# Probabilities times V as one FP32 matmul, new arena sizes, and grouped-query projections evacuated by ScalarE, in a two-layer hybrid encoder

## Chip, cores and metric

One core of one Trainium2 chip runs the whole program. The metric is device microseconds per execution. The kernel before takes 2137.96 us, the median of three runs (2136.34 to 2138.89).

## What is computed

Two groups of tokens (256 of a prompt and 512 of a sample, 768 columns in all) go through two layers with the same weights. Everything is FP32 at the interface. Cut to what matters here:

```python
for l in range(DEPTH):                       # DEPTH = 2, D_MODEL = 1024
    x = x + parallel_mixers(rmsnorm(x, norm_mix_g[l]), w_in[l], ...)    # 16 heads of 64
    x = x + memory_cross_attention(rmsnorm(x, norm_x_g[l]), mem, ...)   # 4 heads, 256 memory tokens
    x = x + conv_ffn(rmsnorm(x, norm_ffn_g[l]), ...)                    # gated MLP, width 2752

# parallel_mixers: 4 heads of dilated attention (A), 4 of mLSTM (B), 8 of grouped-query attention (C)
qc = axial_rope(rmsnorm(heads(c_q, C_HEADS), qk_g[0]), rope_row, rope_col)
kc = axial_rope(rmsnorm(heads(c_k, C_KV_HEADS), qk_g[1]), rope_row, rope_col)
s = einsum('bqkgd,bskd->bkgqs', q, k);  p = softmax(s);  o = einsum('bkgqs,bskd->bqkgd', p, v)
```

## The kernel before

Activations lie with channels on the partitions and the 768 tokens on the free axis. `STREAMS` is the order in which the two groups are worked on: `(256, 512)` first, then `(0, 256)` (first column, count). Almost all matmuls run in the type fp32r with both operands split into a high part (a rounding copy, usually by ScalarE, `hi_op`) and a low part (a DVE subtraction). A projection `proj` (`mm_chunks`, L213 to L215) makes three matmuls for each of 8 weight chunks: high by high, high by low, low by high. Its weights arrive by DMA in `wr` and are split into `wh` (ScalarE) and `wl` (DVE).

A layer is four stages in the program: the mixers, the output projection and cross attention, and the FFN (`up`, `down`; L1105 to L1107 and L1148 to L1150). In the mixers `ahead(first, second)` puts the projections of the next head group beside the attention of the present one; a scheduler that works on priorities and planned durations then sets the order of the instructions on every engine. Each engine takes its own list strictly in that order.

`attend` (L367 to L406) is one head of one group of tokens. Scores go to PSUM bank `s` (L378, L379; two banks), `soft` turns them to probabilities in a 512-column tile of `arena_f`, and PE transposes these 128 by 128 into bank `t` (L392; two banks). Then, for each `t` of 512 columns:

- ScalarE copies `t` to `ph` in fp32r (through L183), and DVE writes `pl` as `t` minus `ph` (through L158). Both lie in a small arena `asm` of 4 x 512 columns.
- PE multiplies by the tokens of V, whose tile holds for each head a [high, low] pair of 64 columns each (the second head of a pair has them the other way round): L400 with `ph`, L401 with `pl`, both into bank `yps`, of which there is one (tag `Y`). So 64 partitions of `yps` collect the high part of V and the other 64 the low part.
- At a head's end ScalarE copies one half of `yps` to the result row block and DVE adds the other half (`xall<-yps` and, in cross attention, `arena_f<-yps`).

There are 184 such `t` in the program. The V tiles come from `v_tokens` (L340 to L353): a transpose into `vps`, then for each of two heads a ScalarE copy (L350) and a DVE subtraction.

Of the grouped-query heads, `c_kv` (L582) and `c_q` (L627) project k and q. DVE evacuates PSUM with one operation (`ev_k`, `ev_q`): times the head's gain, times the row `rbc` of the layer norm (1/rms of each token, spread over the partitions). ScalarE squares the same PSUM for the per-head norm (L635 and L193); `head_rs` makes the reciprocal roots. `ones` and indicator columns multiply FP32 sums of squares on PE in `col_sums` (L268), one matmul for each 128 tokens: `col_sums` on 512 tokens issues four.

Two arenas in SBUF hand out tiles by hand: `arena_r` (fp32r; 18 x 768 columns and the 4 x 512 of `asm`) and `arena_f` (FP32; 18 x 768). A tile that was freed can be taken again, and the new writer waits for the old readers.

Of the kernel before, what the change touches and what calls it, by code (L numbers as in the profile page):

```python
# [44 lines left out]
R_COLS = 18 * 768  # L45
S_COLS = 4 * 512
PREP = 7 * 512
F_COLS = 18 * 768
# [60 lines left out]
def trunk_kernel(ctx, tc, xT, memT, w_in, w_out, w_xq, w_xkv, w_xo, w_up, w_dn, w_dnt, par, fin_g, cst, fmk, tabs,  # L109
# [18 lines left out]
    r_all = ap.tile([128, R_COLS + S_COLS], F32R, name="arena_r")  # L128
    ar = Arena(r_all, R_COLS, T)
    asm = Arena(r_all[:, R_COLS:], S_COLS)  # L130
# [23 lines left out]
    scr_v = nc.dram_tensor("scr_v", (DEPTH, 2, 128, 4 * 2 * 128), F32, kind="Internal").ap()  # L154
# [64 lines left out]
    C_G, A_G, SITE = [0], [0], [""]  # L219
# [147 lines left out]
    def attend(qs, q0, nq, KH, KL, k0, nk, vv, vt0, e, y, y0, soft, settle_p=None):  # L367
# [20 lines left out]
        for kb in range(0, nkt, nb):  # L388
# [17 lines left out]
        tt(yo, yps[64 * e:64 * e + 64, :n], yo, ALU.add)  # L406
# [59 lines left out]
    def kv_proj(l, mh, ml, arena, ftile, first, each=None):  # L466
        for j in range(4):
# [6 lines left out]
            hl = arena.tile(1024)  # L474
# [5 lines left out]
            else:  # L480
                vv = hl.rearrange("p (a b c) -> p a b c", a=2, c=128)
                v_tokens(z, 4, [vv[:, 0], vv[:, 1]], "kv%d" % l)
                SY.dma_start(out=scr_v[l, j - 2], in_=hl.bitcast(F32))
            arena.free(hl)
# [33 lines left out]
    def mixers(l, xt, x_dram, stats):  # L518
# [63 lines left out]
        def c_kv():  # L582
# [4 lines left out]
            def ev_k(ps, c0, n):  # L587
                stt(zk[:, c0:c0 + n], ps, pr[:, l, C_KG:C_KG + 1], rbc[:, c0:c0 + n], ALU.mult, ALU.mult)
# [30 lines left out]
        def v_proj(t):  # L619
            zv = ft()  # L620
            proj(w_in[l, t], xh, xl, ev_to(zv, "v%d" % t), sub="w_v%d" % t)
            vv = [rtl(), rtl()]
            v_tokens(zv, 6, [tok(v) for v in vv], "v%d" % t)
            af.free(zv)
            return vv

        def c_q(g):  # L627
            cosc, sinc = C["cos"], C["sin"]
            zs, sqs = [], []
            for a in range(2):  # L630
                z, sq = ft(), ft()

                def ev_q(ps, c0, n, z=z, sq=sq, a=a):
                    stt(z[:, c0:c0 + n], ps, pr[:, l, C_QG + a:C_QG + a + 1], rbc[:, c0:c0 + n], ALU.mult, ALU.mult)
# [10 lines left out]
            V.tensor_scalar(rq8, rq, 0.125, None, op0=ALU.mult)  # L645
# [23 lines left out]
        def c_attn(g, qr):  # L669
            C_G[0], SITE[0] = g, "c%d" % g  # L670
            qs, rq8 = qr
            K = C["k"][g]
            vv = C["v"][g]
# [6 lines left out]
            ar.free(K, vv)  # L680
# [53 lines left out]
        def b_attn(pb, sv):  # L734
            SITE[0] = "b%d" % pb
            sts, vv, rows = sv
            for e in range(2):
                qs, K = sts[e]
                hd = 2 * pb + e
                for c0, n in STREAMS:  # L740
                    gb = rows[e][:, 2 * c0:2 * c0 + 2 * n].rearrange("p (d k) -> p d k", d=2)
                    attend(qs, c0, n // 128, K[:, :T], K[:, T:], c0, n, tok(vv[e]), c0 // 128, e, yt[5 + pb], c0,
                           *b_soft(gb, c0, n, hd))
                af.free(rows[e])
                ar.free(qs, K, vv[e])
# [77 lines left out]
        def a_attn(pg, sv, order, last=True):  # L823
            A_G[0], SITE[0] = pg, "a%d" % pg
            sts, vv = sv
            for e, (c0, n) in order:
                qs, K = sts[e]
                attend(qs, c0, n // 128, K[:, :T], K[:, T:], c0, n, tok(vv[e]), c0 // 128, e, yt[4 + 3 * pg], c0,
                       mask_soft(C["fm"], den[:, 4 + pg, c0 // 128:(c0 + n) // 128, e]))
            if last:  # L830
                for e in range(2):
                    ar.free(*sts[e], vv[e])
# [611 lines left out]
```

## Time and profile before

| | |
|---|---|
| median of three runs | 2137.96 us |
| the profiled execution | 2145.01 us, of which the span of the trace is 2143.2 us |
| PE busy | 2003.8 us, 93% |
| PE weight loads busy | 1782.8 us, 83% |
| DVE busy | 1841.7 us, 86% |
| ScalarE (ACT) busy | 1061.7 us, 50% |
| granted PE clock, mean | 0.963 |
| chain that ended last | PE 74%, DVE 16%, ACT 4%, DMA 3%, issue 2% |

The profile puts each instruction on its engine's line with a start and a duration. Matmuls are pipelined: a record goes on after the next matmul has begun, so the distance of starts tells what a matmul costs PE, and the duration doesn't. PEclk is the share of the full TensorE clock that was granted. The first layer's mixers and cross attention lie between about 75 and 600 us, its FFN from there to 1085, the second layer's mixers and cross attention from 1085 to 1660, its FFN from 1660 to 2120.

### The profile page before, as it was taken

Reading aid. Unit: us, or ns where it says so; the run is one execution under the profiler, and the core shown is the slowest. Engines: PE = TensorE matmul, PEld = TensorE weight load, DVE = VectorE, ACT = ScalarE, POOL = GpSimd, SP = SyncE. Lnnn points to the kernel's source line nnn. Section 1 sums busy time; section 2 is a strip of 40 time slices with the busy share of each in tenths; the row PEclk is TensorE's granted clock in tenths of the full one; section 3 lists DMA queues with packets and bytes.
Section 4 is the critical chain, followed back from the end, with each engine's and each line's share of the span. In section 5 each row is a group of like instructions: output and inputs, shape, how many; then the busy total and the mean of one; then the engine's idle time right before and its main releaser. Section 6 shows DMA issues by size and latency. Waiting matters only on the chain.

```text
span 2143.2 us, 31059 instructions
## 1 busy us (share of the span) xinstructions
PE 2003.8 (93%) x11280; PEld 1782.8 (83%) x11280; DVE 1841.7 (86%) x3822; ACT 1061.7 (50%) x2119; POOL 7.8 (0%) x32
## 2 busy tenths in 40 slices
PE   7989989998899999999999897999988999999997
PEld 5878768787789999999888775777877999999995
DVE  8787887867999999999977868778779999999998
ACT  4257767547533333333534667565665333333342
POOL 0000000000000000000000000000000000000000
PEclk8989989999999999999999998999999999999998
DMA  5433335342132212212254314343421222222202
GB/s 179 138 82 101 96 89 124 110 132 80 50 90 79 67 62 72 74 63 88 65 179 117 92 44 107 99 111 123 124 64 56 83 70 69 70 69 70 69 30 79
DMA packets 62953, 190.94 MB, mean 89 GB/s; under 512 B 8072, under 2 KB 11400, under 8 KB 62032
## 3 DMA queue, kind: packets, MB, share of 16 engines
q1 hardware_dynamic: 62800, 188.96, 30.1%
q8 instruction: 89, 1.46, 0.3%
q14 instruction: 64, 0.52, 0.1%
HBM read 145.97 MB, written 10.71 MB: 73 GB/s over the span
## 4 chain that ended last, share of the span: by engine, by line
PE 74%; DVE 16%; ACT 4%; DMA 3%; issue 2%; SPq 1%; POOL 0%; DVEq 0%; ACTq 0%
PE rps L1105 8%; PE rps L1107 8%; PE rps L1106 8%; PE rps L1148 5%; PE rps L1149 5%; PE rps L1150 5%; PE prS L213 4%; PE prS L214 4%; PE prS L215 4%; DVE arena_f L158 4%; PE t L392 3%; PE prP L213 2%; PE prP L214 2%; PE prP L215 2%; DVE arena_r L158 2%
## 5 line engine op out<-in xcount | busy, mean ns | idle before, releaser
L158 DVE TENSOR_TENSOR arena_f<-arena_f 128x512 f32<-128x512 f32 (+2 forms) x373 | 265.6, 728 | 27.7 <-DMA arena_f<-arena_f 15.2
L183 ACT CAST wh<-arena_f 128x512 fp32r<-128x512 f32 x266 | 162.2, 621 | 253.0 <-PE rps L1106 212.8
L183 ACT CAST wh<-wr 128x512 fp32r<-128x512 f32 x260 | 159.4, 620 | 236.3 <-PE rps L1106 98.9
L158 DVE TENSOR_TENSOR xall<-rps,xall 128x512 f32<-128x512 f32 (+1 forms) x384 | 197.9, 549 | 14.1 <-PE rps L1150 6.9
L1148 PE MATMUL rps<-arena_r,wh 128*128 128x512 f32 (+1 forms) x608 | 202.6, 339 | 3.4 <-DVE xall L158 3.2
L158 DVE TENSOR_TENSOR wl<-wr,wh 128x512 fp32r<-128x512 f32 x264 | 179.5, 683 | 29.5 <-ACT wh L183 27.9
L1105 PE MATMUL rps<-xha,wh 128*128 128x384 f32 x608 | 203.9, 335 | 0.5 <-ACT wh L183 0.4
L1106 PE MATMUL rps<-xla,wh 128*128 128x384 f32 x608 | 203.4, 335 | 0.0
L1149 PE MATMUL rps<-arena_r,wh 128*128 128x512 f32 (+1 forms) x608 | 201.2, 338 | 0.0
L1107 PE MATMUL rps<-xha,wl 128*128 128x384 f32 x608 | 199.2, 334 | 0.0
L213 PE MATMUL prS<-xha,wh 128*128 128x512 f32 x480 | 188.8, 397 | 3.1 <-DVE arena_f L158 1.0
L215 PE MATMUL prS<-xha,wl 128*128 128x512 f32 x480 | 189.1, 396 | 1.5 <-DVE wl L158 1.5
L214 PE MATMUL prS<-xla,wh 128*128 128x512 f32 x480 | 189.9, 396 | 0.0
L158 DVE TENSOR_TENSOR wl<-arena_f,wh 128x512 fp32r<-128x512 f32 x266 | 179.2, 684 | 1.5 <-ACT wh L183 1.3
L1150 PE MATMUL rps<-arena_r,wl 128*128 128x512 f32 (+1 forms) x608 | 178.3, 339 | 0.0
L158 DVE TENSOR_TENSOR arena_f<-rps,arena_f 128x384 f32<-128x384 f32 x266 | 143.6, 552 | 28.2 <-PE rps L1107 26.0
L1105 PE MATMUL rps<-arena_r,wh 128*128 128x384 f32 x456 | 152.8, 335 | 0.0
L1106 PE MATMUL rps<-arena_r,wh 128*128 128x384 f32 x456 | 152.3, 334 | 0.0
L158 DVE TENSOR_TENSOR arena_r<-t,arena_r 128x512 fp32r<-128x512 f32 x184 | 124.9, 683 | 27.8 <-ACT arena_r L183 24.4
L213 PE MATMUL prP<-xha,wh 128*128 128x256 f32 x480 | 138.9, 289 | 9.8 <-DVE xall L158 5.9
L1107 PE MATMUL rps<-arena_r,wl 128*128 128x384 f32 x456 | 146.4, 334 | 0.0
L392 PE MATMUL t<-cs,arena_f 128*128 128x128 f32 x736 | 125.6, 291 | 13.9 <-DVE arena_r L158 7.5
(235 smaller groups left out, 5004.7 us busy)
## 6 DMA issues: line engine op xcount, KB each, us to landing
arena_f<-in_w_up SPq DMA_DIRECT2D x76, 512.0 KB, 3.6
wr<-in_w_in SPq DMA_DIRECT2D x42, 512.0 KB, 3.6
wr<-in_w_dn SPq DMA_DIRECT2D x40, 512.0 KB, 3.7
wr<-in_w_out SPq DMA_DIRECT2D x32, 512.0 KB, 5.2
arena_r<-arena_r SPq DMA_DIRECT2D x32, 384.0 KB, 6.7
arena_r<-arena_r SPq DMA_DIRECT2D x48, 192.0 KB, 4.0
xall<-in_xT SPq DMA_DIRECT2D x8, 768.0 KB, 8.7
arena_r<-arena_r SPq DMA_DIRECT2D x64, 96.0 KB, 2.2
```

The lines of the kernel that those rows point to most:

```text
L158: V.tensor_tensor(out, a, b, op=op)
L183: A.copy(out, a)
L213: PE.matmul(ps, h[:, j], xh[i][:, c0:c0 + n], start=i == 0, stop=False)
L214: PE.matmul(ps, h[:, j], xl[i][:, c0:c0 + n], start=False, stop=False)
L215: PE.matmul(ps, lo[:, j], xh[i][:, c0:c0 + n], start=False, stop=i == tot - 1)
L392: PE.transpose(t[:, j * n + i * 128:j * n + (i + 1) * 128], ptiles[i][:, (kb + j) * 128:(kb + j + 1) * 128], ident)
L1105: PE.matmul(ps, h[:, k], x[k], start=k == 0, stop=False)
L1106: PE.matmul(ps, h[:, k], x[4 + k], start=False, stop=False)
L1107: PE.matmul(ps, lo[:, k], x[k], start=False, stop=k == 3)
L1148: PE.matmul(ps, h[:, m], hh[i][:, c], start=k == 0 and not tail, stop=False)
L1149: PE.matmul(ps, h[:, m], hlo[i][:, c], start=False, stop=False)
L1150: PE.matmul(ps, lo[:, m], hh[i][:, c], start=False, stop=i == b - 1)
```

## The change

1. In `attend` the probabilities stay FP32: ScalarE copies `t` to one FP32 tile `ph` of `arena_f`, and one FP32 matmul with the 64 columns of V of this head writes 64 partitions of `yps`. The subtraction into `pl`, the second matmul and the final addition of halves are gone.
2. `v_tokens` makes one FP32 copy of a 128-column transpose on ScalarE for both heads; V tiles move to `arena_f` and are half as large, and so is their DRAM scratch for cross attention.
3. `ev_k` and `ev_q` become ScalarE copies that scale by the gain; the norm row is multiplied in where the head roots are spread or scaled (`rc`).
4. `arena_r` has 20 x 768 columns and no `asm`, `arena_f` 18 x 768 + 1024. The FFN's sub-arenas follow these sizes. In `b_attn` the two groups of tokens swap order.

```diff
-R_COLS = 18 * 768
-S_COLS = 4 * 512
+R_COLS = 20 * 768
-F_COLS = 18 * 768
+F_COLS = 18 * 768 + 1024
...
 def v_tokens(zv, nt, vv, site):
-            for e in range(2):
-                src = ps[:, :n].rearrange("p (i h d) -> p i h d", h=2, d=64)[:, :, e]
-                a, b = 64 * e, 64 - 64 * e
-                A.copy(vv[e][:, j0:j0 + m, a:a + 64], src)
-                tt(vv[e][:, j0:j0 + m, b:b + 64], src, vv[e].bitcast(F32)[:, j0:j0 + m, a:a + 64], ALU.subtract)
+            A.copy(vv[:, j0:j0 + m], ps[:, :n].rearrange("p (i d) -> p i d", d=128))
...
 def attend(...):
-            ph, pl = asm.tile(512), asm.tile(512)
-            hi_op(pick("ph_" + SITE[0], "A"), ph, t)
-            tt(pl, t, ph.bitcast(F32), ALU.subtract)
+            ph = af.tile(512)
+            A.copy(ph, t)
             for j in range(nb):
                 kt = kb + j
-                w = vv[:, vt0 + kt]
-                PE.matmul(yps[:, :n], w, ph[:, j * n:(j + 1) * n], start=kt == 0, stop=False)
-                PE.matmul(yps[:, :n], w, pl[:, j * n:(j + 1) * n], start=False, stop=kt == nkt - 1)
-            asm.free(ph, pl)
+                PE.matmul(yps[64 * e:64 * e + 64, :n], vv[:, vt0 + kt, 64 * e:64 * e + 64],
+                          ph[:, j * n:(j + 1) * n], start=kt == 0, stop=kt == nkt - 1)
+            af.free(ph)
         af.free(*held)
-        yo = y[64 * e:64 * e + 64, y0:y0 + n]
-        hi_op(pick("yo_" + SITE[0], "A"), yo, yps[64 - 64 * e:128 - 64 * e, :n])
-        tt(yo, yps[64 * e:64 * e + 64, :n], yo, ALU.add)
+        A.copy(y[64 * e:64 * e + 64, y0:y0 + n], yps[64 * e:64 * e + 64, :n])
...
 def c_kv():
-                stt(zk[:, c0:c0 + n], ps, pr[:, l, C_KG:C_KG + 1], rbc[:, c0:c0 + n], ALU.mult, ALU.mult)
+                A.activation(zk[:, c0:c0 + n], ps, ACT.Copy, scale=pr[:, l, C_KG:C_KG + 1])
...
-                    V.tensor_copy(rtv[:, :, a, e], rk[:, :, e:e + 1].to_broadcast([128, 6, 32]))
+                    tt(rtv[:, :, a, e], rk[:, :, e:e + 1].to_broadcast([128, 6, 32]),
+                       rc[:, :, None].to_broadcast([128, 6, 32]), ALU.mult)
...
 def c_q(g):
-                    stt(z[:, c0:c0 + n], ps, pr[:, l, C_QG + a:C_QG + a + 1], rbc[:, c0:c0 + n], ALU.mult, ALU.mult)
+                    A.activation(z[:, c0:c0 + n], ps, ACT.Copy, scale=pr[:, l, C_QG + a:C_QG + a + 1])
...
-            V.tensor_scalar(rq8, rq, 0.125, None, op0=ALU.mult)
+            stt(rq8, rq, 0.125, rc[:, :, None].to_broadcast([128, 6, 4]), ALU.mult, ALU.mult)
...
 def b_attn(pb, sv):
-                for c0, n in STREAMS:
+                for c0, n in STREAMS[::-1]:
```

Since the scheduler plans the order anew, instructions move on every engine. PE, in the first grouped-query attention of layer 1 (`yps` is the result of probabilities times V, `t` a transpose, `s` scores, `prP` a projection), before:

```order
L401 MATMUL yps<-arena_r 128x512
L400 MATMUL yps<-arena_r 128x512
L392 MATMUL t<-cs,arena_f 128x128 x4
L401 MATMUL yps<-arena_r 128x512
L392 MATMUL t<-cs,arena_f 128x128 x4
L378 MATMUL s<-arena_r 128x512
L379 MATMUL s<-arena_r 128x512
```

and at the same place in the changed kernel (its line numbers are other ones):

```order
L392 MATMUL yps<-arena_f 64x512
L386 MATMUL t<-cs,arena_f 128x128 x2
L392 MATMUL yps<-arena_f 64x512
L386 MATMUL t<-cs,arena_f 128x128 x6
L211 MATMUL prP<-xha,wh 128x256
L212 MATMUL prP<-xla,wh 128x256
L213 MATMUL prP<-xha,wl 128x256
```

One instruction of 64 output partitions stands where two of 128 stood. In the whole program 174 separate runs of such `yps` rows stand between instructions of other shapes.

DVE, a little later in the same attention (`m` is the negated row maximum of scores, `nu` and `nt` head roots, `rq` the scaled roots), before:

```order
L161 SCALAR_TENSOR_TENSOR nu<-nt,nu 128x24
L423 TENSOR_REDUCE m<-s 128x1
L645 TENSOR_SCALAR rq_983<-nu 128x24
L158 TENSOR_TENSOR arena_r<-t,arena_r 128x512
L158 TENSOR_TENSOR m_1218<-m,rq_804 128x1
L158 TENSOR_TENSOR arena_r<-t,arena_r 128x512
L558 TENSOR_SCALAR arena_f<-arena_f 64x768
L423 TENSOR_REDUCE m<-s 128x1
```

and now:

```order
L159 SCALAR_TENSOR_TENSOR nu<-nt,nu 128x24
L159 SCALAR_TENSOR_TENSOR rq_971<-nu,rc 128x24
L156 TENSOR_TENSOR arena_f<-prP,rbc 128x256
L156 TENSOR_TENSOR wl<-wr,wh 128x512
L413 TENSOR_REDUCE m<-s 128x1 x2
L156 TENSOR_TENSOR m_1193<-m,rq_792 128x1
L547 TENSOR_SCALAR arena_f<-arena_f 64x768
```

The two subtractions from `t` that stood between two row maxima are gone, and the maxima follow each other.

## Rows read from the trace of the kernel before

**Rows 1.** Busy us of each engine by stretch; two attention stretches, one FFN

```profile
core 0: us, PE busy (x) PEld busy (x) DVE busy (x) ACT busy (x) POOL busy (x), PEclk, DMA share, GB/s
75.00:600.00 525.00, 480.06 (x2729) 406.48 (x2728) 429.15 (x1031) 325.65 (x729) 3.88 (x14) 0.95 0.36 99
600.00:1085.00 485.00, 479.77 (x2723) 451.93 (x2722) 461.11 (x794) 193.24 (x305) 0.00 (x0) 1.00 0.24 77
1085.00:1660.00 575.00, 516.96 (x2897) 435.26 (x2896) 444.61 (x1078) 333.39 (x748) 3.75 (x14) 0.94 0.35 98
```

**Rows 2.** The chain that ended last, its shares of the stretch 75 to 600

```profile
by line: PE prS L213 7.8%; PE prS L214 7.5%; PE prS L215 7.5%; DVE arena_f L158 6.8%; PE t L392 5.4%; PE prP L213 5.2%; PE prP L214 4.8%; PE prP L215 4.8%; DVE arena_r L158 3.9%; issue 3.3%; PE yps L400 3.2%; PE yps L401 3.1%; DVE xall L158
```

**Rows 3.** PE groups by shape: count, busy us, mean ns, idle before and releaser

```profile
L400 PE MATMUL yps<-arena_r 128*128 128x512 f32 x144 | 65.3, 453 | 7.6 <-ACT arena_r L183 5.4 <-DVE xall L158 2.1
...
L400 PE MATMUL yps<-arena_r 128*128 128x256 f32 x80 | 24.4, 319 | 10.6 <-DVE xall L158 10.1 <-DVE m L423 0.3
...
L276 PE MATMUL bps<-cs,arena_f 128*128 128x128 f32 x12 | 1.6, 272 | 0.0
```

**Rows 4.** Timeline of PE: start us, duration us, instruction; first and last of 15, fp32r, 512 columns

```profile
1499.67 0.39 PE L215 MATMUL prS<-xha,wl 128*128 128x512 f32 x1
...
1502.84 0.39 PE L214 MATMUL prS<-xla,wh 128*128 128x512 f32 x1
```

**Rows 5.** The same view, first and last of six, fp32r of 256 columns

```profile
123.39 0.28 PE L213 MATMUL prP<-xha,wh 128*128 128x256 f32 x1
...
123.98 0.28 PE L215 MATMUL prP<-xha,wl 128*128 128x256 f32 x1
```

**Rows 6.** The same view, FP32: four transposes; sums of squares over 512 tokens

```profile
207.44 0.60 PE L392 MATMUL t<-cs,arena_f 128*128 128x128 f32 x4
...
403.26 1.05 PE L268 MATMUL cps<-cs,arena_f 128*128 128x2 f32 x8 [0.34 <-DVE xall L161]
```

**Rows 7.** DVE groups that the change removes or alters, columns as in Rows 3

```profile
L158 DVE TENSOR_TENSOR arena_r<-t,arena_r 128x512 fp32r<-128x512 f32 x184 | 124.9, 683 | 27.8 <-ACT arena_r L183 24.4 <-PE yps L401 2.4
...
L158 DVE TENSOR_TENSOR xall<-yps,xall 64x512 f32<-64x512 f32 x32 | 22.0, 686 | 4.7 <-ACT xall L183 4.1
...
L158 DVE TENSOR_TENSOR xall<-yps,xall 64x256 f32<-64x256 f32 x32 | 13.3, 417 | 4.9 <-ACT xall L183 4.4
...
L158 DVE TENSOR_TENSOR arena_r<-vps,arena_r 128x256 fp32r<-128x256 f32 x28 | 11.7, 419 | 6.1 <-ACT arena_r L350 5.9
...
L158 DVE TENSOR_TENSOR arena_r<-vps,arena_r 128x128 fp32r<-128x128 f32 x20 | 5.6, 279 | 0.1
...
L161 DVE SCALAR_TENSOR_TENSOR arena_f<-rps,pr,rbc 128x512 f32<-128x512 f32 x6 | 4.4, 728 | 10.3 <-PE rps L215 8.4 <-PE vps L346 2.0
...
L161 DVE SCALAR_TENSOR_TENSOR arena_f<-rps,pr,rbc 128x256 f32<-128x256 f32 x6 | 2.8, 474 | 0.7 <-PE rps L215 0.7
...
L598 DVE COPY arena_f<-nu 128x192 f32<-128x192 f32 x8 | 1.5, 254 | 0.0
```

**Rows 8.** Waits of PE over the whole span: us in total, times, longest us

```profile
PE yps L400 <- DVE xall L158: 12.1, 9, 3.4
...
PE s L378 <- DVE dn L769: 9.5, 9, 3.0
PE t L392 <- DVE arena_r L158: 7.5, 7, 2.2
...
PE yps L400 <- ACT arena_r L183: 5.4, 4, 2.5
```

**Rows 9.** ScalarE groups, columns as in Rows 3

```profile
L183 ACT CAST arena_r<-t 128x512 fp32r<-128x512 f32 x184 | 105.5, 584 | 50.8 <-PE t L392 31.1 <-PE yps L400 17.4 <-DVE nt L161 1.2
...
L185 ACT ACTIVATE xha<-xall,pr 128x512 fp32r<-128x512 f32 x42 | 29.2, 718 | 16.8 <-DVE xall L158 13.2 <-PE prS L215 3.5
...
L185 ACT ACTIVATE xha<-xall,pr 128x256 fp32r<-128x256 f32 x48 | 22.6, 501 | 7.3 <-DVE xall L158 7.3
```

More of the change, by code (lines that the diff above doesn't have):

```diff
@@ L127, in trunk_kernel @@
     af = Arena(f_all, F_COLS)
-    r_all = ap.tile([128, R_COLS + S_COLS], F32R, name="arena_r")
+    r_all = ap.tile([128, R_COLS], F32R, name="arena_r")
     ar = Arena(r_all, R_COLS, T)
-    asm = Arena(r_all[:, R_COLS:], S_COLS)
     ft = lambda n=T: af.tile(n)
@@ L153, in trunk_kernel @@
     scr_k = nc.dram_tensor("scr_k", (DEPTH, 64, 2, 2, 2, 512), F32, kind="Internal").ap()
-    scr_v = nc.dram_tensor("scr_v", (DEPTH, 2, 128, 4 * 2 * 128), F32, kind="Internal").ap()
+    scr_v = nc.dram_tensor("scr_v", (DEPTH, 2, 128, 4 * 128), F32, kind="Internal").ap()
     scr_g = nc.dram_tensor("scr_g", (DEPTH, 36, T), F32, kind="Internal").ap()
@@ L218, in trunk_kernel @@
     turn, wide = [0], [False]
-    C_G, A_G, SITE = [0], [0], [""]
+    C_G, A_G = [0], [0]
     def ps_rot(*tags):
@@ L473, in kv_proj @@
                 each(j)
-            hl = arena.tile(1024)
+            hl = arena.tile(1024) if j < 2 else ftile.tile(512)
             if j < 2:
@@ L480, in kv_proj @@
             else:
[L481 to L484, printed above, removed]
+                v_tokens(z, 4, tok(hl), "kv%d" % l)
+                SY.dma_start(out=scr_v[l, j - 2], in_=hl)
+            (arena if j < 2 else ftile).free(hl)
             ftile.free(z)
@@ L621, in v_proj @@
             proj(w_in[l, t], xh, xl, ev_to(zv, "v%d" % t), sub="w_v%d" % t)
-            vv = [rtl(), rtl()]
-            v_tokens(zv, 6, [tok(v) for v in vv], "v%d" % t)
+            vf = ft()
+            v_tokens(zv, 6, tok(vf), "v%d" % t)
             af.free(zv)
-            return vv
+            return vf
         def c_q(g):
@@ L669, in c_attn @@
         def c_attn(g, qr):
-            C_G[0], SITE[0] = g, "c%d" % g
+            C_G[0] = g
             qs, rq8 = qr
             K = C["k"][g]
-            vv = C["v"][g]
+            vv = C["v"]
             for hh in range(4):
@@ L679, in c_attn @@
                 ar.free(qs[hh])
-            ar.free(K, vv)
+            ar.free(K)
+            if g:
+                af.free(vv)
         def stacks(qq, kk):
@@ L739, in b_attn @@
                 hd = 2 * pb + e
-                for c0, n in STREAMS:
+                for c0, n in STREAMS[::-1]:
                     gb = rows[e][:, 2 * c0:2 * c0 + 2 * n].rearrange("p (d k) -> p d k", d=2)
-                    attend(qs, c0, n // 128, K[:, :T], K[:, T:], c0, n, tok(vv[e]), c0 // 128, e, yt[5 + pb], c0,
+                    attend(qs, c0, n // 128, K[:, :T], K[:, T:], c0, n, tok(vv), c0 // 128, e, yt[5 + pb], c0,
                            *b_soft(gb, c0, n, hd))
                 af.free(rows[e])
-                ar.free(qs, K, vv[e])
+                ar.free(qs, K)
+            af.free(vv)
         def b_soft(gb, c0, n, hd):
@@ L823, in a_attn @@
         def a_attn(pg, sv, order, last=True):
-            A_G[0], SITE[0] = pg, "a%d" % pg
+            A_G[0] = pg
             sts, vv = sv
@@ L827, in a_attn @@
                 qs, K = sts[e]
-                attend(qs, c0, n // 128, K[:, :T], K[:, T:], c0, n, tok(vv[e]), c0 // 128, e, yt[4 + 3 * pg], c0,
+                attend(qs, c0, n // 128, K[:, :T], K[:, T:], c0, n, tok(vv), c0 // 128, e, yt[4 + 3 * pg], c0,
                        mask_soft(C["fm"], den[:, 4 + pg, c0 // 128:(c0 + n) // 128, e]))
@@ L831, in a_attn @@
                 for e in range(2):
-                    ar.free(*sts[e], vv[e])
+                    ar.free(*sts[e])
+                af.free(vv)
         ths = []
@@ L933, in cross @@
         for j in range(2):
-            vt = rtl(1024)
-            SY.dma_start(out=vt.bitcast(F32), in_=scr_v[l, j])
+            vt = ft(512)
+            SY.dma_start(out=vt, in_=scr_v[l, j])
             K = rtl(2048)
@@ L946, in queries @@
         def queries(c0, n, k0, vt0):
-            SITE[0] = "x%d" % n
             xh, xl = split_x(xt, gx, "sx", ((c0, n),))
@@ L964, in queries @@
                 vt, K = kvs[j]
-                vv = vt.rearrange("p (a b c) -> p a b c", a=2, c=128)
+                vv = tok(vt)
                 for e in range(2):
@@ L999, in cross @@
         b = queries(cp, np_, 0, 0)
-        for p in kvs:
-            ar.free(*p)
+        for v, k in kvs:
+            af.free(v)
+            ar.free(k)
         d = new_norm()
@@ L1012, in ffn @@
         _, rbc = stats
-        rf = Arena(r_all, R_COLS + S_COLS, T)
+        rf = Arena(r_all, R_COLS, T)
         fp = Arena(f_all[:, :2 * PREP], 2 * PREP)
```

3 lines of the change are left out of this document (1 added, 2 removed).

## Prediction

> **What bounds the kernel now.** I read the table of busy times by stretch first, then the chain, then PE's groups with their starts, then DVE's groups, then PE's waits. The table [rows 1] shows two kinds of stretch. In the FFN PE is busy for 479.8 of 485 us and has no room. In the two stretches of mixers and cross attention no engine is full: PE is busy for 480 of 525 and 517 of 575 us, so 45 + 58 = 103 us idle, while DVE has 429 and 445 us (82% and 77%) and ScalarE 326 and 333 (60%). The granted clock there is 0.95 and 0.94. Its levels are 2.4 and 1.2 GHz, so about 10% of 525 and 12% of 575 us, some 121 us, ran at the lower one. The chain [rows 2] says that PE leads there too, with DVE's pieces between: the products with V (L400 and L401) are 6.3% of 525 us, 33 us, and `arena_r` through L158, which holds the subtractions, 3.9%. So there PE has the most work and DVE makes it wait. The change takes work from the second and gives work to the first. The question is the exchange rate.
>
> **What PE gets.** In dense stretches an fp32r matmul of 512 columns starts 0.226 us after the last (3.17 us in 14 steps) [rows 4], one of 256 columns after 0.118 (0.59 us in 5 steps) [rows 5]. Now, 144 pairs of the first and 80 of the second [rows 3] cost 144 x 0.452 + 80 x 0.236 = 84 us. For plain FP32 there is no row with a wide operand, but two rows say how it goes. Four FP32 transposes of 128 columns take 0.60 us together, of which the last alone is 0.27 [rows 6, 3]: (0.60 - 0.27) / 3 = 0.11 us for 128 columns, nearly what 256 columns of fp32r cost, so FP32 columns pass at half the rate. And where sums over 512 tokens are four FP32 matmuls in the program, the trace has eight records [rows 6]: each FP32 product that is no transpose goes through PE twice. Both together: 512 columns cost 2 x 4 x 0.11 = 0.88 us and 256 columns 0.44, which makes 144 x 0.88 + 80 x 0.44 = 162 us, or **78 us more**. The low end is nothing (only one of the two doublings holds for wide operands: 0.44 in place of 0.452); a gain is excluded, since both rows cost at least as much for each column as the pair of fp32r. I take 78, since both doublings are seen. Of the products' 42 us in the first stretch (half of 84) the chain holds 33, 78%; so **61 us** lie on the path and 17 fall into waits of PE.
>
> **What DVE loses** [rows 7]. Subtractions from `t`: 184 x 0.683 = 126 us. Final additions: 40 x 0.686 + 40 x 0.417 = 44 (the 16 of cross attention, on `arena_f`, priced like the 64 on `xall`). Low parts of V: 28 x 0.419 + 20 x 0.279 = 17. Evacuations of the grouped-query projections: 10 x 0.728 + 10 x 0.474 = 12. Together **199 us**, 23% of the 874 that DVE works in the two stretches. Eight copies of 254 ns become multiplications of the same shape, and four tiny scalings get a second operand: nothing, hidden by DVE's free time; without it 8 x 0.25 = 2 us at most.
>
> What this is worth on the path has three parts.
> - PE's waits for what goes: for the addition that empties the only `yps` bank 12.1 us, for the subtraction that empties `t` 7.5, for `ph`, whose small arena frees a tile only when L400 and L401 have read it, 5.4 [rows 8]. Sum **25 us**, which is also the low end. The copy from `yps` by ScalarE stays, and is what is late next.
> - The other waits. Of 103 us idle, 78 are left. About 18 of these I leave out as tied to transfers and row broadcasts (an estimate from PE's waits, of which the largest that stays is the 9.5 for the sums of mLSTM [rows 8]). DVE's free share rises from 18% to some 37%, so an operation that queues behind others queues about half as long: half of 60, **30 us**. Ends: 0 and 60.
> - The clock. If all 121 us at half clock were matmuls, 60 us were lost. Fewer waits, and a longer product, keep PE at work; I take a quarter, **15 us**, between 0 and 30.
>
> **Edits to ScalarE, queues and memory.** Twenty evacuations come to ScalarE: 10 x 0.72 + 10 x 0.50 = 12 us by its nearest scaled copies [rows 9]; V's 48 half copies become 24 whole ones, a little less. At 60% busy this is covered. Uncovered it is the last evacuation before each per-head norm that counts: three a layer, 6 x (0.72 + 0.50) = 7 us at most, since the square now queues behind the scaled copy. Against that, evacuation no longer waits for `rbc`. I take nothing. SP issues the same number of transfers; those of V's scratch shrink to half. `ph` now comes from `arena_f` and need not wait for two small pairs. The FFN's arenas shift by some hundred columns; its stretches are PE's, so nothing.
>
> **The sum.** 61 - 25 - 30 - 15 = **-9 us**. The profiled execution took 2145.0 us, 7 above the median of 2138.0; against the median the forecast is **2129 us**. By its ends: 2138 - 25 - 60 - 30 = 2023 with free FP32, 2138 + 78 - 25 = 2191 with nothing else gained.
>
> **The rivals.**
> - *PE becomes the bound* (slower). PE already leads in these stretches, and idle time that comes from the shape of the program (norms, rotations, stacked operands through DMA, the first head of a group) doesn't care how busy DVE is. Then the 30 and 15 us don't come: 61 - 25 = +36, **2174 us**. It decides from the point at which the other waits and the clock give back less than 36 us. For it: FFN, where DVE is busy for 461 of 485 us and PE still doesn't wait [rows 1], so a busy DVE alone is no reason to wait. Against it: the order there is regular, and in attention DVE's lists mix long and urgent work.
> - *A change of shape costs PE its pipeline* (slower). The products with V now use 64 output columns of the array, all others 128, and 174 runs of them stand in the order. If PE emptied itself at both ends of each run, that would cost up to the part of a record that overlaps the next matmul, 0.39 - 0.226 = 0.16 us [rows 4]: 174 x 2 x 0.16 = 56 us, **2185 us**. The Trainium skill has this rule (TensorEngine Tiling (Array Packing), Key Properties): a change of tiling mode drains TensorE. No row of this trace has a 64-column product, so none bears it out yet.
> - *FP32 costs PE nothing more* (faster). If a wide FP32 product passed at half rate once, the 61 us go: **2068 us**. The half rate is in the rows; the two records for each product speak against it. The Trainium skill can be read this way (Perfetto Trace Analysis, Engine Utilization): its footnote halves TensorE's peak for FP32_LOW_HIGH. Its page FP8 and Floating Point Precision (TensorE Precision Notes) counts four passes for true FP32, which is what two records at half rate make; the trace agrees with the second.
> - *Nothing that can be measured*: the new order gives back what it gains, **2138 us**.
>
> **How the numbers follow.** A measurement of this kernel can tell about 0.2% (4.3 us) from no change. Forecast 0.40, PE the bound 0.30, change of shape 0.08, free FP32 0.10, nothing 0.12. The forecast's own range is 2105 to 2145, so of its 0.40 I count 0.36 as faster, 0.02 as same, 0.02 as slower. Faster: 0.36 + 0.10 = 0.46. Same: 0.12 + 0.02 = 0.14. Slower: 0.30 + 0.08 + 0.02 = 0.40. The range has to reach to both sides: up to 2186 it holds all of the rival in which PE is the bound and half of the change of shape, down to 2078 the forecast with its larger gains and the part of free FP32 in which little else is won.
>
> **What would show it.** In the changed profile the `yps` group should still have 448 records (224 products, two records each), those of 512 columns 0.44 us apart; 0.22 apart would mean free FP32. DVE should be busy for some 1640 us, and its groups on `t`, `yps` and `vps` be gone. PE's idle in the two attention stretches should fall from 103 to about 50 us with a granted clock of 0.96 or more; if it stays above 75 us, PE is the bound with waits that DVE didn't cause. Gaps of 0.1 us or more before and after each run of `yps` that no semaphore ends would show the change of shape. The FFN stretches should keep their 485 and 460 us; if they don't, the new order or the arenas did something that I left out, and the forecast is right or wrong for another reason.

## The result and the profile after

The changed kernel takes **2196.1 us**, the median of four runs (2194.89 to 2197.35); the kernel before, in the same comparison, 2138.43 (2136.34 to 2144.28). The ratio is 1.0265, 95% interval [1.0244, 1.0287]: slower by 58 us, where 9 us less were forecast. The time lies just above the range.

The page's busy times of the changed kernel, then the row of the clock in slices:

```profile
span 2195.4 us, 30512 instructions
...
PE 2089.0 (95%) x11280; PEld 1736.3 (79%) x11280; DVE 1682.6 (77%) x3490; ACT 1066.6 (49%) x2115; POOL 7.8 (0%) x32
...
PEclk8999999999999999999999999999999999999998
```

PE has 85 us more than the 2003.8 of before, DVE 159 less, and PE's idle time, span less busy, fell from 139 to 106 us. So DVE was relieved, PE waits less, its mean clock rose from 0.963 to 0.979, and yet the span grew by 52 us. What grew is PE's own work, by more than the 74 us of the new product's columns (worked out below).

Where? Cutting the span at the first and last product with V of each layer gives the two stretches of attention. Busy times by stretch, before:

```profile
125.00:540.00 415.00, 377.02 (x2139) 316.86 (x2139) 330.48 (x825) 275.53 (x631) 3.78 (x13) 0.94 0.37 100
1168.00:1598.00 430.00, 382.96 (x2149) 319.34 (x2148) 329.15 (x823) 275.66 (x633) 3.65 (x13) 0.94 0.35 97
```

and the same stretches of work in the changed kernel (columns as in rows 1):

```profile
125.00:570.00 445.00, 418.59 (x2139) 293.18 (x2139) 258.60 (x677) 275.99 (x623) 3.78 (x13) 0.98 0.35 92
1201.00:1649.00 448.00, 422.40 (x2140) 294.45 (x2140) 255.94 (x670) 274.99 (x623) 3.68 (x14) 0.97 0.34 92
```

30 + 18 = 48 of the 52 us lie here. PE's idle time fell from 38 + 47 = 85 us to 26 + 26 = 52, but its busy time rose by 42 + 39 = 81. What lies between (the FFN of layer 1 and the projections of layer 2) took 628 us and takes 631, so neither the FFN nor its new arenas have a part in it.

The chain of the second of these stretches, its shares by line, before and then in the changed kernel:

```profile
by line: PE prS L213 8.2%; PE prS L214 8.1%; PE prS L215 8.0%; PE t L392 6.0%; DMA arena_r<-arena_r 4.7%; PE prP L213 4.3%; PE prP L214 4.2%; PE prP L215 4.1%; DVE arena_f L158 4.0%; PE s L378 3.9%; DVE arena_r L158 3.8%; PE yps L400 3.8%; 
...
by line: PE yps L392 19.2%; PE t L386 9.5%; PE prS L211 9.2%; PE prS L212 9.0%; PE prS L213 8.9%; PE prP L211 4.6%; PE prP L213 4.3%; PE s L372 4.2%; PE prP L212 4.2%; PE s L373 3.7%; DVE arena_f L156 2.3%; DMA arena_r<-arena_r 2.1%; DMA ar
```

The products with V are 19.2% of 448 us, 86 us, where L400 was 3.8% of 430 us and L401 at most as much (the line breaks off there), together 33 us or less. DVE's pieces between PE's have shrunk: L158 was 4.0% and 3.8% for the two arenas, its successor is 2.3% for `arena_f`.

The groups of the product with V, where [rows 3] stood, with busy us, mean ns and idle before:

```profile
L392 PE MATMUL yps<-arena_f 128*64 128x512 f32 x288 | 156.9, 633 | 4.0 <-ACT arena_f L389 3.8
...
L392 PE MATMUL yps<-arena_f 128*64 128x256 f32 x160 | 43.1, 392 | 1.4 <-ACT arena_f L389 1.4
```

448 records as forecast, two for each product. Waits that end with ScalarE's copy `ph` are 5 us in all, and the waits for DVE's addition and subtraction [rows 8] are gone. The copy, where [rows 9] stood, is as long as before and waits for transposes alone:

```profile
L389 ACT COPY arena_f<-t 128x512 f32<-128x512 f32 x184 | 103.7, 584 | 62.3 <-PE t L386 61.1
```

PE's largest waits now are for other work (us in total, times, longest):

```profile
PE t L386 <- ACT arena_f L423: 14.3, 4, 6.6
PE bps L314 <- ACT arena_f L309: 8.4, 4, 3.5
PE prP L211 <- DVE arena_f L156: 7.7, 6, 2.2
```

The timeline of PE shows what no wait shows. One run of products in the changed kernel (start, duration, instruction):

```profile
199.93 0.39 PE L213 MATMUL prS<-xha,wl 128*128 128x512 f32 x1
200.25 1.08 PE L392 MATMUL yps<-arena_f 128*64 128x256 f32 x4
201.26 0.51 PE L211 MATMUL prS<-xha,wh 128*128 128x512 f32 x1
201.60 0.38 PE L386 MATMUL t<-cs,arena_f 128*128 128x128 f32 x2
```

`L213` has 512 columns of fp32r, which cost 0.226 us in a dense stretch [rows 4]; here the next instruction starts 0.32 us later, with nothing shown that it waits for. The four records of 256 columns should cost 0.86; the next matmul starts after 1.01. Over the whole trace, a record of 512 FP32 columns inside a run starts 0.429 us after the last, one of 256 columns 0.216. The record ahead of a run costs 0.09 more than in a dense stretch, the first record of the run 0.05 more, and the last 0.09 more. Gaps of this kind, of 0.1 us, were the prediction's sign for the change of shape.

The weight loads (PEld) of the same piece show what is missing:

```profile
199.70 0.19 PEld L213 LDWEIGHTS prS<-xha,wl 128*128 128x128 f32 x1
200.25 0.62 PEld L392 LDWEIGHTS yps<-arena_f 128*64 128x64 f32 x4 [0.36 <-issue]
201.26 0.19 PEld L211 LDWEIGHTS prS<-xha,wh 128*128 128x128 f32 x1 [0.39 <-issue]
```

The weights of `L213` are loaded from 199.70 on, 0.23 us ahead of its matmul, while the matmul before it runs. Those of the first product with V are loaded only from 200.25 on, when its matmul starts, and those of `L211` behind the run only from 201.26 on. Over all runs without a wait, the load begins in the median 0.002 us ahead of the matmul at either end of a run. So at each change of shape PE does not load weights beside the matmul that runs. Why it doesn't, no row tells.

### The profile page after: what moved, and what is told of

It is laid out like the page before. It is cut to its first block, busy times and chain, and to the rows that moved or that the text cites. A ratio compares the mean times of both kernels' runs of the same rounds, so it can differ in the third digit from the quotient of the medians.

```text
span 2195.4 us, 30512 instructions
## 1 busy us (share of the span) xinstructions
PE 2089.0 (95%) x11280; PEld 1736.3 (79%) x11280; DVE 1682.6 (77%) x3490; ACT 1066.6 (49%) x2115; POOL 7.8 (0%) x32
## 5 line engine op out<-in xcount | busy, mean ns | idle before, releaser
L156 DVE TENSOR_TENSOR arena_f<-arena_f 128x512 f32<-128x512 f32 (+3 forms) x373 | 267.2, 731 | 25.3 <-DMA arena_f<-arena_f 8.0
L156 DVE TENSOR_TENSOR xall<-rps,xall 128x256 f32<-128x256 f32 (+1 forms) x384 | 200.6, 552 | 19.7 <-PE rps L1143 8.7
L1100 PE MATMUL rps<-xha,wl 128*128 128x384 f32 x608 | 203.8, 335 | 2.5 <-DVE wl L156 2.4
L392 PE MATMUL yps<-arena_f 128*64 128x512 f32 (+1 forms) x448 | 200.0, 547 | 5.4 <-ACT arena_f L389 5.2
L211 PE MATMUL prS<-xha,wh 128*128 128x512 f32 x480 | 190.9, 401 | 5.1 <-DVE arena_f L156 3.7
L213 PE MATMUL prS<-xha,wl 128*128 128x512 f32 x480 | 189.4, 396 | 0.4 <-DVE wl L156 0.4
L1143 PE MATMUL rps<-arena_r,wl 128*128 128x512 f32 (+1 forms) x608 | 182.8, 339 | 0.8 <-DVE wl L156 0.8
L386 PEld LDWEIGHTS t<-cs,arena_f 128*128 128x128 f32 x736 | 84.3, 143 | 121.8 <-issue 89.8
L211 PE MATMUL prP<-xha,wh 128*128 128x256 f32 x480 | 142.0, 296 | 11.6 <-DVE arena_f L156 5.8
```

The costliest lines, as they stand in the source:

```text
L156: V.tensor_tensor(out, a, b, op=op)
L211: PE.matmul(ps, h[:, j], xh[i][:, c0:c0 + n], start=i == 0, stop=False)
L213: PE.matmul(ps, lo[:, j], xh[i][:, c0:c0 + n], start=False, stop=i == tot - 1)
L392: PE.matmul(yps[64 * e:64 * e + 64, :n], vv[:, vt0 + kt, 64 * e:64 * e + 64], ph[:, j * n:(j + 1) * n], start=kt == 0, stop=kt == nkt - 1)
L1100: PE.matmul(ps, lo[:, k], x[k], start=False, stop=k == 3)
L1143: PE.matmul(ps, lo[:, m], hh[i][:, c], start=False, stop=i == b - 1)
```

## Experiments

**Theory 1** from here on: the columns cost what was forecast, and the loss comes from the change of shape, from 128 output columns to 64 and back, at each of the 174 runs. Its rival: PE had become the bound, and relieving DVE was worth little.

**e1: the FP32 product 128 columns wide.** Both heads of the pair are multiplied and one half is thrown away; moving columns, records, DVE and ScalarE stay as in the changed kernel.

```diff
-                PE.matmul(yps[64 * e:64 * e + 64, :n], vv[:, vt0 + kt, 64 * e:64 * e + 64],
+                PE.matmul(yps[:, :n], vv[:, vt0 + kt],
```

> The changed kernel, with one edit: the FP32 product with V uses all 128 columns of a V tile (both heads) and writes all 128 partitions of yps; the copy still takes this head's 64. Theory 1 (the shape costs PE): in the changed profile each run of 64-column products has a matmul before it that starts its successor 0.09 us late, a first record of 0.48 instead of 0.43 us and a last record after which the next starts 0.52 instead of 0.43 us later, 0.24 us for each of 174 runs, 41 us in all. Without the change of shape I expect 30 to 41 us back: 2155 to 2166 us, and all records 0.43 us apart. Theory 2 (PE is the bound whatever the shape, FP32 rate alone explains the loss): 2185 to 2200 us.

Measured: 2135.28 us (2132.38 to 2136.39), ratio to before 0.9959 [0.9941, 0.9977]. By medians 61 us of the loss are gone, by ratios 66, more than theory 1 expected. The same piece of the program as above, in this kernel's timeline:

```profile
194.76 0.39 PE L213 MATMUL prS<-xha,wl 128*128 128x512 f32 x1
194.99 1.02 PE L392 MATMUL yps<-arena_f 128*128 128x256 f32 x4
195.66 0.59 PE L211 MATMUL prS<-xha,wh 128*128 128x512 f32 x1
196.09 0.38 PE L386 MATMUL t<-cs,arena_f 128*128 128x128 f32 x2
```

From `L213` to `L386` it takes 1.33 us, with 64 columns 1.67: **0.34 us for one run**. Part of the price falls behind the run's last record, in the matmul that follows, and is missed by whoever looks at the gaps alone. So I took, for every run, the time from the start of the record before it to the start of the third record behind it, less its columns at full clock. The median is 0.316 us with 64 columns and 0.026 with 128 where transposes follow (some 120 and 110 runs), and 0.397 and 0.057 where an fp32r matmul follows (some 35 each): 0.29 and 0.34 us for a run, some 0.30 x 174 = 52 us. The weight load of the first product begins here 0.12 us (median) ahead of its matmul, where it began 0.002 us ahead with 64 columns. The attention stretches of this kernel:

```profile
125.00:539.00 414.00, 393.06 (x2132) 313.07 (x2131) 256.12 (x672) 272.56 (x620) 3.78 (x13) 0.98 0.37 99
1172.00:1590.00 418.00, 396.76 (x2142) 315.24 (x2142) 255.33 (x670) 274.26 (x623) 3.65 (x14) 0.97 0.36 98
```

PE's busy time is 25 us less in each than with 64 columns, its idle time 5 us less (21 + 21).

**e6: changes of shape without columns.** To e1, one FP32 product with 64 output columns and a single moving column is added ahead of each head's first product; the real product overwrites what it leaves.

```diff
+            if kb == 0:
+                PE.matmul(yps[64 * e:64 * e + 64, :1], vv[:, vt0, 64 * e:64 * e + 64], ph[:, :1], start=True, stop=True)
```

> The wide FP32 product (e1) with one additional FP32 product of 64 output columns and a single moving column ahead of each head's first product; what it writes is overwritten. That puts 80 changes of shape into the order and next to no columns. Theory shape (it is the change to and from 64 columns that costs, 0.24 us by the spacing of records and 61 / 174 = 0.35 us by the whole difference): 80 x 0.24 to 80 x 0.35, so 19 to 28 us over e1, 2154 to 2164 us, with the same 0.09 us ahead of each and 0.09 us behind. Rival (the change of shape costs nothing by itself, the 61 us came from the order or from the 64-column products as such): at most 80 x 2 records x 0.03 = 5 us over e1, 2135 to 2141 us.

Measured: 2153.39 us (2151.92 to 2158.55), ratio 1.0053 [1.0036, 1.0071]. Against e1's 0.9959 that is 0.0094 x 2142 = 20 us for 80 changes, 0.25 us each (2142 us is about the middle of the medians of the kernel before, 2138 to 2145). By ratios this lies inside the 19 to 28 us that theory 1 expected; the median itself, 18 us over e1, lies just under. In its timeline two transposes precede the additional pair of records:

```profile
203.79 0.38 PE L344 MATMUL vps<-cs,arena_f 128*128 128x128 f32 x2
204.10 0.28 PE L391 MATMUL yps<-arena_f 128*64 128x1 f32 x2
204.31 1.13 PE L394 MATMUL yps<-arena_f 128*128 128x512 f32 x2
205.27 0.38 PE L386 MATMUL t<-cs,arena_f 128*128 128x128 f32 x2
```

Two transposes cost 0.22 us in a dense stretch (0.11 each, [rows 6]) and 0.31 here. The pair costs 0.21, and the two records of 512 columns behind it take 0.96 where 0.86 is their price: 0.09 + 0.21 + 0.10 = 0.40 us of PE, all told.

The time alone does not decide here, since the rival was priced too low. The eight records of `L268` in [rows 6] have the full shape and two columns; the next matmul of the kernel before stands at

```profile
404.17 0.48 PE L400 MATMUL yps<-arena_r 128*128 128x512 f32 x1
```

so they cost 0.91 us, 0.11 each and not 0.03. By this, an additional product of full shape, two such records, would have cost 0.22 us too (an estimate), and eighty of them 18 us, about what was measured. A run with 80 full-shape products was not made. What e6 does show is in the rows: 0.19 of the 0.40 us lie ahead of the pair and behind it, where a change of shape puts them, and 0.21 are what a small product costs anyhow.

**e9, e10, e11: the 64 columns elsewhere in the array.** Three variants of the changed kernel, in which only the half of `yps` that is written differs (the copy reads from there): always partitions 0 to 63, always 64 to 127, and the halves of even and odd heads exchanged.

```diff
-yps[64 * e:64 * e + 64, :n]
+yps[0:64, :n]
...
-yps[64 * e:64 * e + 64, :n]
+yps[64:128, :n]
...
-yps[64 * e:64 * e + 64, :n]
+yps[64 - 64 * e:128 - 64 * e, :n]
```

> The changed kernel, but every product with V writes partitions 0 to 63 of yps, for the even and the odd head of a pair alike, and ScalarE copies from there. The 64 columns stay, only their place in the array no longer alternates. Theory width (it is the step between 128 and 64 columns that costs, wherever the 64 lie): as the changed kernel, 2190 to 2202 us, with 0.09 us ahead of a run and 0.09 us behind. Rival place (columns 64 to 127 cost, columns 0 to 63 don't): half of the 61 us go, about 2165 us, and the gaps are gone from all runs.

> The changed kernel, but every product with V writes partitions 64 to 127 of yps, for both heads of a pair. With all of them in partitions 0 to 63 (e9) the time was 2167 us at the same price of a run, and the scheduler had set another order (2883 of 11280 PE records stand elsewhere than in the changed kernel). Theory order (each run costs the same 0.29 us wherever its columns lie, and the scheduler's new order is worth up to some 30 us of waits, by chance of the plan): an order of its own again, anywhere from 2160 to 2205 us, with the same 0.29 us for each run. Rival place (columns 64 to 127 are dearer): all heads pay now what half of them pay in the changed kernel, 2196 + 29 = about 2225 us.

> The changed kernel with the halves of yps exchanged: even heads write partitions 64 to 127, odd heads 0 to 63. As many products lie in each half as in the changed kernel, and they alternate as there. Theory order: another plan, so another time, between 2160 and 2205 us, and the same price of a run. Rival place or alternation (the halves, or the step between them, cost PE itself): as the changed kernel, 2193 to 2199 us.

Measured: e9 2167.26 us (ratio 1.0110 [1.0082, 1.0138]), e10 2191.57 (1.0216 [1.0201, 1.0232]), e11 2185.37 (1.0191 [1.0174, 1.0208]). e9 alone looked like the rival "place": half of the loss gone. But its runs cost what they cost in the changed kernel (medians 0.318 and 0.400 us); in e9's timeline:

```profile
197.61 0.39 PE L213 MATMUL prS<-xha,wl 128*128 128x512 f32 x1
197.93 1.08 PE L392 MATMUL yps<-arena_f 128*64 128x256 f32 x4
198.94 0.51 PE L211 MATMUL prS<-xha,wh 128*128 128x512 f32 x1
199.28 0.38 PE L386 MATMUL t<-cs,arena_f 128*128 128x128 f32 x2
```

1.67 us again. And e10, which by "place" had to be at 2225, is faster than the changed kernel. What differs is the scheduler's order, which comes out differently for each choice of half: compared place by place (line, tiles and shape of the PE records), 2251 of 11280 differ between e9 and the changed kernel, and only 335 between e9 and e1 (the 2883 of e10's expectation is another count of the same). So e1 and e9 are a pair with nearly one order and two widths: 32 us by medians, for 165 runs at 0.30 = 50 us on PE. And the four kernels with 64 columns are four orders at one width: 2167, 2185, 2192 and 2196 us, a spread of 29 us.

**e12 and e5: other orders of the wide product.** Which of the two is the price of the shape, 32 or 61 us, depends on whether e1 was lucky. e12 is e1 with part 4's swap of token groups undone; e5 is e1 with part 3 undone (DVE evacuates the grouped-query projections again, and the norm row is multiplied there).

```diff
-                for c0, n in STREAMS[::-1]:
+                for c0, n in STREAMS:
```

> The changed kernel with the wide FP32 product (e1) and the mLSTM attention's groups of tokens in the order of the kernel before: a third plan for the 128-column product, beside e1 (2135 us) and e5 (2132 us). The four plans with 64 columns gave 2167, 2185, 2192 and 2196 us. Theory A (the plans scatter by chance around a level which the price of the runs sets, some 174 x 0.30 = 52 us lower for the wide product): 2125 to 2155 us, below all four. Rival B (e1 and e5 were lucky plans, and the price of the runs is only the 32 us between e1 and e9): 2150 to 2165 us.

```diff
-                A.activation(zk[:, c0:c0 + n], ps, ACT.Copy, scale=pr[:, l, C_KG:C_KG + 1])
+                stt(zk[:, c0:c0 + n], ps, pr[:, l, C_KG:C_KG + 1], rbc[:, c0:c0 + n], ALU.mult, ALU.mult)
...
-                    A.activation(z[:, c0:c0 + n], ps, ACT.Copy, scale=pr[:, l, C_QG + a:C_QG + a + 1])
+                    stt(z[:, c0:c0 + n], ps, pr[:, l, C_QG + a:C_QG + a + 1], rbc[:, c0:c0 + n], ALU.mult, ALU.mult)
```

> The changed kernel with the FP32 product written 128 columns wide (e1) and, besides, the evacuations of the grouped-query projections given back to DVE (part 3 undone). What is left of the change is the exchange of 78 us of PE for some 187 us of DVE, and the arenas. Theory 1 (the gains add up: part 3 is worth the 10 us that it is worth on the kernel before): e1 plus 8 to 12 us, 2143 to 2148 us, no better than the kernel before. Rival (part 3 is worth something only while DVE is as full as before; after the change DVE has room): within 3 us of e1, 2133 to 2138 us.

Measured: e12 2138.23 us (2135.99 to 2140.10), ratio 0.9979 [0.9968, 0.9990]; e5 2131.57 (2129.07 to 2132.76), 0.9945 [0.9928, 0.9962]. Three orders with 128 columns have a mean ratio of 0.9961, four with 64 columns 1.0196. **The difference is 0.0235 x 2142 = 50 us**, what 174 runs at 0.30 us cost (52). e1 was not lucky. The profiles say where the price lies (idle is the span less PE busy):

| kernel | columns | runs of products | PE busy, us | PE idle, us | granted clock |
|---|---|---|---|---|---|
| changed | 64 | 174 | 2089.0 | 106 | 0.979 |
| e10 | 64 | 179 | 2085.5 | 105 | 0.983 |
| e11 | 64 | 174 | 2084.6 | 98 | 0.981 |
| e9 | 64 | 165 | 2074.5 | 89 | 0.982 |
| e12 | 128 | 165 | 2034.7 | 101 | 0.980 |
| e1 | 128 | 165 | 2036.3 | 98 | 0.976 |
| e5 | 128 | 168 | 2035.2 | 94 | 0.979 |

PE is busy for 48 us longer with 64 columns (means 2083.4 and 2035.4), and idle for as long as with 128 (100 and 98). So the price is PE's own time and not a matter of waits. The pair e9 and e1 fits this too: 38 us more busy and 9 us less idle. The clock of e9 was 0.982 against 0.976, some 25 us less at the half clock, worth up to 12 us if all of them were matmuls (an estimate); 38 + 12 is the 50 us of 165 runs. The changed kernel, at 1.0265, lies some 0.007 x 2142 = 15 us above the mean of its kind, about 6 in PE's busy time and 7 in its idle time; its order is the likely reason, not tested by itself. For part 3, e5 lies 3 us under e1, on the side of its rival; with three wide orders 7 us apart, that says only that part 3 is worth little here.

**e2: the kernel before without DVE's part.** The subtraction into `pl` and the final addition are left out; the second product reads `ph` again, so PE's work is the same. The result lacks the low part of the probabilities, counts the rounded ones double, and keeps one half of `yps`.

```diff
-            tt(pl, t, ph.bitcast(F32), ALU.subtract)
...
-                PE.matmul(yps[:, :n], w, pl[:, j * n:(j + 1) * n], start=False, stop=kt == nkt - 1)
+                PE.matmul(yps[:, :n], w, ph[:, j * n:(j + 1) * n], start=False, stop=kt == nkt - 1)
...
-        tt(yo, yps[64 * e:64 * e + 64, :n], yo, ALU.add)
```

> The kernel before, with PE's work unchanged (both products with V stay, both read the high part of the probabilities) and DVE's part taken away: no subtraction from t, no final addition (the low part of the probabilities and of V are left out of the result). It prices what relief of DVE is worth by itself, 170 us of DVE work in the attention stretches. Theory 1 (the gain was about 57 us, since 74 us of FP32 and 41 us of shape were paid and 58 us were lost): 2075 to 2095 us. Theory 2 (DVE hardly held the kernel up, only the 25 us of waits seen on removed work): 2110 to 2130 us.

Measured: 2083.19 us (2082.18 to 2085.67), ratio 0.9716 [0.9698, 0.9734]: **60 us** for 126 + 44 = 170 us of DVE's instructions. PE was the busiest engine and still lost 60 us to DVE. The rival "PE becomes the bound", which had granted 25 us, falls. The 60 include what the clock gave, which rose from 0.963 to 0.974.

**e3: the kernel before with part 3 alone** (the lines of e5's diff, the other way round, and `rc` multiplied into the roots).

```diff
-                stt(zk[:, c0:c0 + n], ps, pr[:, l, C_KG:C_KG + 1], rbc[:, c0:c0 + n], ALU.mult, ALU.mult)
+                A.activation(zk[:, c0:c0 + n], ps, ACT.Copy, scale=pr[:, l, C_KG:C_KG + 1])
...
-            V.tensor_scalar(rq8, rq, 0.125, None, op0=ALU.mult)
+            stt(rq8, rq, 0.125, rc[:, :, None].to_broadcast([128, 6, 4]), ALU.mult, ALU.mult)
```

> The kernel before with the third part of the change alone: grouped-query projections evacuated by ScalarE, the norm row multiplied in at the head roots. Theory 1 (worth little, 12 us of DVE work moved to an engine with room): 2131 to 2139 us. Rival (the square that queues behind the scaled copy on ScalarE delays the roots, three times a layer): 2139 to 2146 us.

Measured: 2132.67 us (2130.07 to 2136.94), ratio 0.9955 [0.9937, 0.9972], some 10 us less, by one plan. That 12 us of DVE's work are worth this while DVE is full, and nothing once it is relieved (e5 against e1), fits both runs but isn't shown: orders of one kernel differ by as much.

**e4: the price of FP32 itself.** The changed kernel with one fp32r product, 128 columns wide; V and `ph` are rounded to fp32r in `arena_r`. The low parts of both are left out of the result.

```diff
-            ph = af.tile(512)
+            ph = ar.tile(512)
...
-                PE.matmul(yps[64 * e:64 * e + 64, :n], vv[:, vt0 + kt, 64 * e:64 * e + 64],
+                PE.matmul(yps[:, :n], vv[:, vt0 + kt],
```

> The changed kernel with the products with V as one fp32r product of 128 columns: V tiles and probabilities are rounded to fp32r and lie in the other arena, low parts of both are left out. PE's work on them falls from 158 + 41 us to 42 us, DVE's and ScalarE's work stays as in the changed kernel. Theory 1 (PE's work is on the path nearly in full): 2196 - 0.8 to 1.0 x 157 = 2039 to 2070 us. Theory 2 (PE's added work mostly lies in waits that were there anyway): 2080 to 2130 us.

Measured: 2056.19 us (2054.76 to 2059.69), ratio 0.9591 [0.9572, 0.9610]. Its products cost 144 x 0.226 + 80 x 0.118 = 42 us of PE, e1's 158: 116 us less on PE gave 79 us of time, 68%.

**e7: the swapped groups of tokens alone**, on the kernel before.

```diff
-                for c0, n in STREAMS:
+                for c0, n in STREAMS[::-1]:
```

> The kernel before with nothing but the swapped order of the two groups of tokens in the mLSTM attention (of part 4). All theories: a few us either way, 2134 to 2146 us. If it is more than 8 us off the kernel before, the order of the groups has a share in the result that the forecast left out, and e1 has to be read with it.

Measured: 2145.24 us (2140.70 to 2150.06), ratio 1.0014 [1.0001, 1.0026]. 2082 of 11280 PE records differ place by place, and the time went up by 3 us: part 4's swap explains nothing here.

**e8: rounded probabilities, exact V.** e3 with the product of `ph` and the [high, low] pair alone; the low part of the probabilities is left out of the result.

```diff
-            tt(pl, t, ph.bitcast(F32), ALU.subtract)
...
-                PE.matmul(yps[:, :n], w, ph[:, j * n:(j + 1) * n], start=kt == 0, stop=False)
-                PE.matmul(yps[:, :n], w, pl[:, j * n:(j + 1) * n], start=False, stop=kt == nkt - 1)
+                PE.matmul(yps[:, :n], w, ph[:, j * n:(j + 1) * n], start=kt == 0, stop=kt == nkt - 1)
```

> The kernel before with ScalarE's evacuations (e3), and probabilities only in their rounded fp32r form: one product with the [high, low] pair of V, no second product, no subtraction from t. The low part of the probabilities is left out of the result; the final addition of halves stays. PE loses half of 84 us, DVE 126 us. Theory 1 (78% of PE's time on the path, and DVE's relief worth what it is worth without the PE change: 60 us for 170, so some 40 for 126): e3 less 33 less 40, about 2060 us, 2045 to 2080. Rival (PE is the bound, the relief of DVE no longer counts once PE leads): e3 less 33 to 42, 2090 to 2100 us.

Measured: 2083.06 us (2082.28 to 2083.87), ratio 0.9720 [0.9702, 0.9738]: 50 us less than e3, between what theory 1 expected and its rival. Taking 42 us from PE and 126 from DVE at once gives less than e2, which took 170 from DVE alone. So the prices of PE's and DVE's time found one at a time are not to be added. That each in part removes the same time is the likely reason; each price here rests on one plan.

## Why the prediction was wrong

- **The step that failed** is the sum itself, in which the change of shape has no term. It stood among the rivals, priced at 174 x 2 x 0.16 = 56 us and held for likely at 0.08, because no row of the trace before had a 64-column product. The runs show 0.29 to 0.34 us for a run, 50 us for the mean of the orders and 61 us between the changed kernel and e1. The price was nearly right. The Trainium skill states the rule (TensorEngine Tiling (Array Packing), Key Properties: changing the tiling mode drains TensorE) and gives no duration; that a run costs time ahead, inside and behind agrees with it. The rows of the new order had shown ahead of any run that 174 runs of 64 columns stood alone between others. A term that a rule names and a count multiplies belonged into the sum with both bounds, 0 and 56.
- **A row for it was there.** The kernel before has two runs of small matmuls on 36 rows of the array in place of 128 (`gps`, L574), another change of shape. That of layer 2, at full clock:

```profile
1196.54 0.39 PE L379 MATMUL s<-arena_r 128*128 128x512 f32 x1
1196.87 0.94 PE L574 MATMUL gps<-cs,arena_f 36*128 36x36 f32 x12
1197.73 0.50 PE L401 MATMUL yps<-arena_r 128*128 128x512 f32 x1
1198.07 0.39 PE L400 MATMUL yps<-arena_r 128*128 128x512 f32 x1
```

`L379` ahead costs 0.33 us in place of 0.226, `L401` behind 0.34. The twelve records between, 0.063 us apart inside, take 0.87, 0.11 over their price. That is 0.1 + 0.11 + 0.11 = 0.32 us for one run, what a run of 64 columns costs.

- **PE's FP32 columns: right.** 288 x 0.429 + 160 x 0.215 = 158 us against the 162 forecast; both doublings hold. 78% of that was put on the path; e4 shows 68% between e1 and one fp32r product, an exchange over another distance.
- **DVE's relief: right.** With the clock, 25 + 30 + 15 = 70 us were forecast for 199 us of instructions; e2 gives 60 for 170, the same share, its clock included. The forecast of 1640 us busy was off (1683): the groups' durations that went do add up to 199, but neighbouring records overlap, so that busy time fell only by 159.
- **The clock** went the way that was forecast, 0.94 to 0.97 and 0.98 in the attention stretches. Over the whole span the time at the lower level fell from some 159 us (0.963) to 92 (0.979); at most half of the difference, 33 us, can have been won. What the 15 us for it are was not measured apart.
- **The sum without shapes holds:** -9 us forecast; the three wide kernels have 0.9961 x 2142 - 2142 = -8. That the terms meet so well is partly luck: with 68% of 158 - 84 = 74 us on the path (50) and DVE's relief at e2's rate (70) the sum would be -20, and e8 warns that they don't simply add.
- **ScalarE's evacuations at nothing: not refuted.** Beside the wide product they make -3 us (e5), on the kernel before 10 (e3), both within what another order may do.
- **The scheduler's order** was taken as part of the terms. It is a cause of its own: 29 us between four orders of the 64-column kernel, which the range did not count. The changed kernel lies 10 us above the range's upper end, and 15 above the mean of its kind. Three orders of the wide kernel scatter by 7 us and two of the kernel before by 3. Why those with 64 columns scatter more, I leave open; four and three orders are few.
- **PE's idle time** was to fall from 103 to about 50 us in the stretches of mixers and cross attention; from the first to the last product with V it fell from 85 to 52, 33 of the 53 us. So a good part of DVE's relief came there, and the rival "PE becomes the bound", in which it would have stayed, gave a time near the result (2174) for a reason that e1 and e2 refute.

The fastest kernel with all of the arithmetic is e5, the FP32 product 128 columns wide with DVE's evacuations: 0.55% under the kernel before, 3.1% under the changed one by their ratios. e3, the kernel before with part 3, is as fast (0.45% under, the intervals overlap). Where rounded operands are enough, e4 is 4.1% under the kernel before.

## What to carry over

When a change makes a matmul narrower than its neighbours in the array, count the runs of it in the order of instructions and charge some 0.3 us for each; filling the array with columns that are thrown away cost nothing here: a record of 512 moving columns takes 0.43 us with 64 and with 128 output columns. Look in the trace before for any run of another shape, whatever it computes; here it had the price. Before an added instruction is taken to price an effect, find what a like instruction costs without the effect. Price an exchange between two engines by one run that takes each side alone, and don't add two such prices without a third run. Where a scheduler plans the order, compare several orders of each kind before a difference of 1% is given a cause.

## What was not expected of the hardware

A run of 64-column products among 128-column ones costs 0.09 us ahead of it, 0.05 in its first record, 0.09 behind its last, and the rest in the matmul behind, 0.29 us before a transpose and 0.34 before an fp32r matmul. It does not depend on which half of the array is used (medians 0.316, 0.318, 0.315 and 0.317 us in the changed kernel, e9, e10 and e11 where transposes follow). A run on 36 rows in the kernel before costs 0.32 us. A product of a single column (e6) loses 0.09 ahead and 0.10 behind as well.

The page names no releaser for it, the records ahead are no longer than before, and PE counts as busy all the while. It shows in the distance of starts, and in the weight loads: at both ends of such a run the load begins with its matmul, not beside the matmul before.

A small FP32 product isn't free: its two records of full shape cost PE 0.11 us each with two moving columns ([rows 6]).
